# A bidirectional hybrid layer on one core: v by column halves for both token blocks, and the output stage's norms one group ahead

## The chip, the cores and the metric

The kernel runs on one NeuronCore of a Trainium2 chip. The metric is device time in microseconds from the start to the end of one launch on that core; lower is better. TensorE is called PE below, VectorE DVE, ScalarE ACT, GpSimd POOL; SP is the engine that issues most transfers.

## What is computed

One encoder layer on a sequence of 2048 tokens of width 1024, in float32:

```
mod = silu(c) @ w_ada + b_ada;  shift, scale, gate = split(mod)
h = rms_norm(x, norm_g) * (1 + scale) + shift
a, a_glu, a_gate, u, v, b_gate = split(h @ W_in)            # 6 x 1024 columns
y_a = silu(layer_norm(conv31(a * sigmoid(a_glu)) + conv_b)) * silu(a_gate)
y_b = u * (W_s @ layer_norm(v) per chunk of 128 tokens and head + b_s) * silu(b_gate)
out = rms_norm(x + gate * (concat(y_a, y_b) @ w_out), final_g)
```

The layer norm of v runs over all 1024 columns of v; the spatial gate then takes, for each of 8 heads, 128 columns of the normalised v.

## The kernel before

**Precision.** Every float32 operand of the large products is split in two parts, a high one and the rest (`split`: ACT copies to the high part, DVE subtracts), and a product is three matmuls: high by high, high by low, low by high. Each of them is 128x128 by 512 columns. 5664 such matmuls are the body of the program: 768 for v, 3360 for the other five column groups of `W_in`, 1536 for `w_out`.

**Halves and pieces.** The sequence is worked in two halves of 1024 tokens (`hf` 0 and 1), each in two token blocks of 512 (r = 0, 1, also called B0 and B1 of x). From the normalised h, the kernel makes seven combined pieces `H` (names A11, A12, S1, A22, S2, S3, S4, each for k = 0 to 3), and a product of two columns by two token blocks takes seven products of a quarter of the size instead of eight (`unit`, the order of M1 to M7 in `ORDER`). v is not made that way: `v_half` makes it with the tokens on the partitions, from A11 and A12 for r = 0, and from S1 and A22 for r = 1, with the weights B1, B2 and Bd = B2 - B1.

**The opening.** 16 tiles `wa` of 512 KB give shift and scale (`mod_half`, one DVE instruction over 128x1024 for each tile, three buffers of the pool `e`); x of half 0 is squared, summed over rows (`x_rows0`, matmul `pc_x`), and spread over the partitions (`spread`, matmul `pr_x`); `h_scale` and `h_parts` make the pieces H. All of it stands ahead of v's first matmul in the order of PE: both `pc_x` and both `pr_x`.

**v before.** `v_half` runs r = 0 with all 1024 columns in eight banks of PSUM, then r = 1. The weights are loaded, split, written back to DRAM (`dW`), and read again wherever they are used a second time. At a block's end, ACT copies four tiles of v to ring slots, DVE and ACT make mean and variance, ACT normalises four tiles of 128x1024 in place (L327), and four writes of 512 KB go to `dV`. In `gmlp`, head j reads its 128 columns of all eight tiles (`vc`, one buffer, 512 KB) and uses them as matmul weights (`px`).

**The middle.** Units `conv_in`, `gmlp` and `conv_gate` follow for each half. The convolution (`conv`) is 736 DVE instructions, L435, set behind everything else by a low priority; those of half 1 run on into the output stage. Its result goes to `dC`.

**The output stage.** Five groups of token tiles, `GROUPS` (0, 3), (3, 4), (7, 4), (11, 3), (14, 2): first tile and number of tiles. The half of the sum over y_b (called B here, weights `wr_8` to `wr_15`) comes first for groups 1 to 4, its partial sums go to DRAM (`part_out`, `dP`). Group 0 then does B and A in one go (`by_rows`), with the weights `wr_0` to `wr_7` replacing those of B; then groups 1 to 4 do A from the partial sums (`part_in`) tile by tile (`by_tile`), and `out_tile` applies gate, residual and the last norm. The conv layer norm of a group is a generator, `norm(gi)`, in four steps: load and sum `Y`; matmul `pmean`, subtract, square; matmul `pc`, reciprocal root; matmul `pr_cn`, scale, Silu (L551), times the gate. In the loop over groups 1 to 4 the norm of group gi + 1 is run while group gi's tiles are multiplied:

```
        if gi + 1 < len(GROUPS):
            steps.append(norm(gi + 1))
        ys = [y_a(gi, j) for j in range(KC)]
        for t in range(nt):
            ...
            step()
        while steps:
            step()
```

**What sets the order.** Each engine runs its own instructions in order; a scheduler at build time merges the program's pieces by priority into one order for each engine, and an instruction that waits holds up those behind it on its engine. Buffers come from pools: `ct` 4 buffers of 256 KB, `e` 3 of 512 KB, `ring` 8, `raw` 2, and in the output stage `ys` 10.

Of the kernel before, what the change touches and what calls it, by code (L numbers as in the profile page):

```python
# [39 lines left out]
def hybrid_layer_kernel(  # L40
# [126 lines left out]

    def mod_half(k, i):
# [3 lines left out]
        w = ek(f"wa_{k}_{i}")  # L172
        nc.sync.dma_start(w, wa_ss[i * KC + k])
# [21 lines left out]
    def x_rows0(xs, rows, b, fills):  # L195
# [72 lines left out]
    def v_op(typ, k, g, name):  # L268
        key = (typ, k, g)
        s = slot(f"w{name}_{typ}_{k}_{g}")  # L270
        if key in dW:
            nc.sync.dma_start(flat(s), dW[key])
            return s
        part = lambda i: w_v[g, 2 * i + k // 2][:, (k % 2) * NG : (k % 2 + 1) * NG]
        raw = ct(f"rv_{typ}_{k}_{g}")
        nc.sync.dma_start(raw, part(0 if typ == "B1" else 1))
        if typ == "Bd":
            r1 = ct(f"rv1_{k}_{g}")
            nc.sync.dma_start(r1, part(0))
            TT(out=raw, in0=raw, in1=r1, op=ALU.subtract)  # L280
        split(s, raw)
        keep(key, s)
        return s

    def v_half(hf, between=lambda: None):
        for r, pairs in enumerate(((("A11", "B1"), ("A12", "B2")), (("S1", "B1"), ("A22", "Bd")))):
            name = f"v{hf}{r}"
            ps = [[(bank if 2 * t + g < 6 else xbank)(f"pv_{hf}_{r}_{t}_{g}") for g in range(2)] for t in range(4)]
            for k in range(KH):
                for i, (b, typ) in enumerate(pairs):  # L290
                    for g in range(2):
                        s = v_op(typ, k, g, name)
                        st, sp = (k, i) == (0, 0), (k, i) == (KH - 1, 1)
                        for t in range(4):
                            a0, a1 = (H[b, k][:, q, t * P : (t + 1) * P] for q in range(2))
                            nc.tensor.matmul(ps[t][g], a0, s[:, 0, :], start=st, stop=False)  # L296
                            nc.tensor.matmul(ps[t][g], a0, s[:, 1, :], start=False, stop=False)  # L297
                            nc.tensor.matmul(ps[t][g], a1, s[:, 0, :], start=False, stop=sp)  # L298
            if r == 0:
                between()  # L300
            st = sm(f"vst_{name}", 16)
            sums, mean, var = st[:, 0:8], st[:, 8:12], st[:, 12:16]
            sq = sm(f"vsq_{name}", 8)
            vt = []
            for t in range(4):
                v = flat(slot(f"vt_{name}_{t}"))
                for g in range(2):
                    act(v[:, g * NG : (g + 1) * NG], ps[t][g], AF.Copy, accum_out=sums[:, 4 * g + t : 4 * g + t + 1])
                vt.append(v)
# [244 lines left out]
    def yslot(name, n):  # L554
        return ysp.tile([P, 2, NG], F32R, tag="ys", name=name)[:, :, :n]
# [123 lines left out]
    for k in range(KH):  # L679
        x_load(0, xs, k, B0)  # L680
# [219 lines left out]
```

## Time and profile before

| | us |
|---|---|
| median of 2 runs | 1459.81 (1458.77 to 1460.85) |
| the profiled execution | 1461.0 |
| its span, first to last instruction | 1459.2 |
| PE, DVE, ACT busy | 1363.8, 1174.6, 545.6 |
| first matmul of v | 43.5 |
| first matmul of the first unit | 147.5 |
| end of the last matmul, start of the last evacuation | 1451.1 |

The page of the profile gives busy time by engine. Matmuls are pipelined, each shown at some 390 ns, while in a stretch without any gap they start every 228 ns, so a stretch's loss is read by counting its matmuls. The view of stages gives busy time and number of instructions of each engine in a stretch; the view of waits names what an idle engine waited for; the timeline shows instructions in order.

### The profile page before, as it was taken

Reading aid. Unit: us, or ns where it says so; the run is one execution under the profiler, and the core shown is the slowest. Engines: PE = TensorE matmul, PEld = TensorE weight load, DVE = VectorE, ACT = ScalarE, POOL = GpSimd, SP = SyncE. Lnnn points to the kernel's source line nnn. Section 1 sums busy time; section 2 is a strip of 40 time slices with the busy share of each in tenths; the row PEclk is TensorE's granted clock in tenths of the full one; section 3 lists DMA queues with packets and bytes.
Section 4 is the critical chain, followed back from the end, with each engine's and each line's share of the span. In section 5 each row is a group of like instructions: output and inputs, shape, how many; then the busy total and the mean of one; then the engine's idle time right before and its main releaser. Section 6 shows DMA issues by size and latency. Waiting matters only on the chain.

```text
span 1459.2 us, 17680 instructions
## 1 busy us (share of the span) xinstructions
PE 1363.8 (93%) x6036; PEld 1120.7 (77%) x6036; DVE 1174.6 (80%) x1976; ACT 545.6 (37%) x989; POOL 33.7 (2%) x82
## 2 busy tenths in 40 slices
PE   2879999999999999999999999999889999997786
PEld 1667788888888888878888888887668888885675
DVE  7972679999999999866898897967998993477864
ACT  4471733444344443542112222222342341345533
POOL 0000000000000000000000000000000000000000
PEclk9999999999999999999999999999999999998898
DMA  8968897869898897669777999999976348355521
GB/s 291 332 246 295 314 393 273 317 238 375 282 345 293 314 309 263 230 224 379 247 233 252 345 389 376 356 366 331 327 279 241 109 163 325 104 187 174 167 97 68
DMA packets 139851, 395.72 MB, mean 271 GB/s; under 512 B 14897, under 2 KB 49873, under 8 KB 135666
## 3 DMA queue, kind: packets, MB, share of 16 engines
q1 hardware_dynamic: 133618, 369.68, 70.9%
q0 software_dynamic: 6144, 24.93, 4.7%
q8 instruction: 47, 0.77, 0.2%
q14 instruction: 42, 0.34, 0.1%
HBM read 234.65 MB, written 159.91 MB: 270 GB/s over the span
## 4 chain that ended last, share of the span: by engine, by line
PE 87%; DVE 5%; DMA 3%; ACT 3%; issue 1%; SPq 0%; DVEq 0%; ACTq 0%
PE pq_u L363 9%; PE pq_a L363 9%; PE po L593 8%; PE po L594 8%; PE po L595 8%; PE pt_u L363 6%; PE pp_u L363 6%; PE pp_a L363 6%; PE pt_a L363 6%; PE pq_s L363 4%; PE pv L296 3%; PE pv L297 3%; PE pv L298 3%; PE pt_s L363 3%; PE pp_s L363 3%; PE px L484 2%
## 5 line engine op out<-in xcount | busy, mean ns | idle before, releaser
L435 DVE SCALAR_TENSOR_TENSOR acc<-gc,cw_sb,acc 128x496 f32<-128x496 f32 (+1 forms) x496 | 345.9, 745 | 0.7
L593 PE MATMUL po<-wr,y 128*128 128x512 f32 x512 | 206.3, 404 | 29.3 <-ACT y L132 23.7
L594 PE MATMUL po<-wr,y 128*128 128x512 f32 x512 | 204.1, 400 | 0.0
L435 DVE SCALAR_TENSOR_TENSOR acc<-gc,cws,acc 128x496 f32<-128x496 f32 (+1 forms) x240 | 179.7, 749 | 29.1 <-ACT acc L444 25.2
L595 PE MATMUL po<-wr,y 128*128 128x512 f32 x512 | 197.3, 393 | 0.0
L593 PEld LDWEIGHTS po<-wr,y 128*128 128x128 f32 x512 | 99.5, 194 | 54.1 <-ACT y L132 25.8
L594 PEld LDWEIGHTS po<-wr,y 128*128 128x128 f32 x512 | 99.3, 194 | 21.7 <-issue 1.0
L595 PEld LDWEIGHTS po<-wr,y 128*128 128x128 f32 x512 | 97.1, 190 | 21.0 <-issue 0.5
L363 PE MATMUL pq_a<-H_S,w_a_M 128*128 128x512 f32 x384 | 92.9, 390 | 1.1 <-ACT w_a_M L132 1.1
L363 PE MATMUL pq_u<-H_S,w_u_M 128*128 128x512 f32 x384 | 93.7, 391 | 0.0
L363 PE MATMUL pt_u<-H_S,w_u_M 128*128 128x512 f32 x384 | 93.5, 391 | 0.0
L363 PE MATMUL pp_a<-H_A,w_a_M 128*128 128x512 f32 x384 | 92.8, 390 | 0.0
L363 PE MATMUL pp_u<-H_A,w_u_M 128*128 128x512 f32 x384 | 92.5, 390 | 0.0
L363 PE MATMUL pt_a<-H_S,w_a_M 128*128 128x512 f32 x384 | 92.2, 389 | 0.0
L363 PEld LDWEIGHTS pq_a<-H_S,w_a_M 128*128 128x128 f32 x384 | 71.8, 188 | 16.7 <-ACT w_a_M L132 1.5
L363 PEld LDWEIGHTS pt_a<-H_S,w_a_M 128*128 128x128 f32 x384 | 72.1, 188 | 15.0
L363 PEld LDWEIGHTS pp_u<-H_A,w_u_M 128*128 128x128 f32 x384 | 71.9, 188 | 14.9
L363 PEld LDWEIGHTS pp_a<-H_A,w_a_M 128*128 128x128 f32 x384 | 71.8, 188 | 14.9 <-ACT w_a_M L132 0.2
L363 PEld LDWEIGHTS pq_u<-H_S,w_u_M 128*128 128x128 f32 x384 | 71.6, 188 | 14.6
L363 PEld LDWEIGHTS pt_u<-H_S,w_u_M 128*128 128x128 f32 x384 | 71.5, 188 | 14.6
L133 DVE TENSOR_TENSOR w_a_M<-raw_a,w_a_M 128x512 fp32r<-128x512 f32 x56 | 37.8, 688 | 22.3 <-ACT w_a_M L132 21.9
L132 ACT ACTIVATE w_u_M<-raw_u 128x512 fp32r<-128x512 f32 x56 | 34.1, 628 | 53.2 <-issue 14.1
(224 smaller groups left out, 2303.8 us busy)
## 6 DMA issues: line engine op xcount, KB each, us to landing
wv_B<-dW_B SPq DMA_DIRECT2D x32, 512.0 KB, 5.8
dW_o<-ws SPq DMA_DIRECT2D x16, 1024.0 KB, 7.2
wr<-dW_o SPq DMA_DIRECT2D x16, 1024.0 KB, 8.8
wa<-in_wa_ss_dram SPq DMA_DIRECT2D x16, 512.0 KB, 5.7
dW_B<-wv_B SPq DMA_DIRECT2D x16, 512.0 KB, 5.0
raw_a<-in_w_main_dram SPq DMA_DIRECT2D x16, 512.0 KB, 6.3
dV<-vt_v SPq DMA_DIRECT2D x16, 512.0 KB, 7.5
dG<-g SPq DMA_DIRECT2D x16, 512.0 KB, 6.2
```

The costliest lines, as they stand in the source:

```text
L132: act(s[:, 0, :], src, AF.Copy)
L133: TT(out=s[:, 1, :], in0=src, in1=s[:, 0, :].bitcast(F32), op=ALU.subtract)
L296: nc.tensor.matmul(ps[t][g], a0, s[:, 0, :], start=st, stop=False)
L297: nc.tensor.matmul(ps[t][g], a0, s[:, 1, :], start=False, stop=False)
L298: nc.tensor.matmul(ps[t][g], a1, s[:, 0, :], start=False, stop=sp)
L363: mm = lambda w, a, st, sp: nc.tensor.matmul(ps, w, a, start=st, stop=sp, skip_group_check=True)
L435: STT(out=pairs(acc, h), in0=pairs(g[:, i : i + n], at), scalar=tab[:, j, i : i + 1], in1=pairs(acc, h), op0=ALU.mult, op1=ALU.add,)
L484: nc.tensor.matmul(ps[:, t * P : (t + 1) * P], vch[:, 4 * b + t, :], wsj, start=True, stop=True)
L593: nc.tensor.matmul(ps, yh, hi, start=st, stop=False, skip_group_check=True)
L594: nc.tensor.matmul(ps, yh, lo, start=False, stop=False, skip_group_check=True)
L595: nc.tensor.matmul(ps, yl, hi, start=False, stop=sp, skip_group_check=True)
```

## The change

Four parts.

1. **Opening.** Ten of the `wa` tiles get buffers of their own (places of H pieces that are not yet in use), so their loads no longer wait for one of three buffers; the four for k = 0 and 4 and the first weights of v are loaded before B1 of x. `x_rows0` for B1 and the pieces of r = 1 are made between the pieces of r = 0, and v's matmuls are interleaved with them.
2. **v.** For each half of the columns (g = 0, 1), both token blocks run at once in eight banks, in the order (r, k) = (0,0), (0,1), (1,0), (0,2), (1,1), (0,3), (1,2), (1,3). B1, B2 and Bd of a (k, g) are made together from two loads, and used for both blocks. v leaves PSUM unnormalised through a `ct` buffer, is squared there against its mean over 512 columns, and goes to `dV` in pieces of 256 KB. Mean and variance over 1024 columns are put together at the end in `vstat`, and `gmlp` normalises `vc` after it is read: eight ACT instructions of 128x128.
3. **Output stage.** B starts with group 3 by rows, then groups 1, 2, 4, then 0. `wr_8` and `wr_9` are loaded into `raw` buffers before the last unit ends. The norm of a group is run one group earlier: norm(2) during group 0's A, norm(gi + 2) during group gi.
4. **Buffers and queues.** `Y` has its own pool of 8, `pi` one of 2, `ys` is 4, and the first four y of a group take ring slots; the write of a partial sum is issued by ACT instead of SP. Tiles other than the last run j-major, both halves of the columns in turn.

```diff
+    def wa_tile(k, i):
+        if (k, i) not in was:
+            if wa_homes:
+                w = hpool.tile([P, D], F32, tag=wa_homes.pop(0), name=f"wa_{k}_{i}")
+            else:
+                w = ek(f"wa_{k}_{i}")
+            nc.sync.dma_start(w, wa_ss[i * KC + k])
...
+    def v_ops(hf, k, g):
...
+        raw = [ct(f"rv{i}_{k}_{g}") for i in range(2)]
+        for i in range(2):
+            nc.sync.dma_start(raw[i], w_v[g, 2 * i + k // 2][:, (k % 2) * NG : (k % 2 + 1) * NG])
+        out = ss()
+        for i in range(2):
+            split(out[i], raw[i])
+        TT(out=raw[1], in0=raw[1], in1=raw[0], op=ALU.subtract)
+        split(out[2], raw[1])
...
+    def v_half(hf):
...
+        for g in range(2):
+            for n, (r, k) in enumerate(((0, 0), (0, 1), (1, 0), (0, 2), (1, 1), (0, 3), (1, 2), (1, 3))):
+                yield
...
+                for t in range(4):
+                    c = 8 * g + 4 * r + t
+                    v = ct(f"v_{hf}_{r}_{t}_{g}")
+                    act(v, ps[r][t], AF.Copy, accum_out=sums[:, c : c + 1])
+                    nc.sync.dma_start(dV[hf][4 * r + t].rearrange("p j d -> p (j d)")[:, g * NG : (g + 1) * NG], v)
+                    nm = sm(f"vnm_{hf}_{c}", 1)
+                    TS(out=nm, in0=sums[:, c : c + 1], scalar1=-1.0 / NG, scalar2=None, op0=ALU.mult)
+                    act(junk, v, AF.Square, bias=nm, accum_out=sqs[:, c : c + 1])
...
-                act(vt[t], vt[t], AF.Identity, bias=nmr[:, t : t + 1], scale=rs[:, t : t + 1])
-                nc.sync.dma_start(dV[hf][4 * r + t].rearrange("p j d -> p (j d)"), vt[t])
...
@@ gmlp
+        for t in range(NTT):
+            act(vch[:, t, :], vch[:, t, :], AF.Identity, bias=vstat[:, 8 + t : 9 + t], scale=vstat[:, t : t + 1])
...
@@ norm
-            y = slot(f"Y_{gi}_{k}", n).bitcast(F32)
+            y = Yp.tile([P, 2, NG], F32, tag="Y", name=f"Y_{gi}_{k}")[:, :, :n]
...
+    def yslot(name, j, n):
+        return slot(name, n) if j < KH else ysp.tile([P, 2, NG], F32R, tag="ys", name=name)[:, :, :n]
...
+            home = (rawp, "raw") if e % KC < 2 else (wrp, f"wr_{e % KC}")
...
-    ysp = pool("ys", 10, reuse_waits="tile")
+    ysp = pool("ys", 4, reuse_waits="tile")
...
@@ by_rows
+            if j % 2 == 0:
+                step()
...
@@ part_out
-        nc.sync.dma_start(dP[t], st)
+        nc.scalar.dma_start(dP[t], st)
...
-    steps += [norm(0), norm(1)]
-    for n, gi in enumerate((1, 2, 3, 4)):
+    for n, gi in enumerate((3, 1, 2, 4)):
...
+        if n == 0:
+            ps = [banks(t0 + t) for t in range(nt)]
+            by_rows(gi, ps, KC, ys, True, True)
+            for t in range(nt):
+                part_out(t0 + t, ps[t])
+            steps += [norm(0), norm(1)]
+            continue
...
-    by_rows(0, ps, 0, y_a, False, True)
+    ys = [y_a(0, j) for j in range(KC)]
+    steps.append(norm(2))
+    by_rows(0, ps, 0, ys, False, True)
...
-        if gi + 1 < len(GROUPS):
-            steps.append(norm(gi + 1))
         ys = [y_a(gi, j) for j in range(KC)]
+        if gi + 2 < len(GROUPS):
+            steps.append(norm(gi + 2))
...
-        while steps:
-            step()
+        if gi + 1 < len(GROUPS):
+            while gi + 1 in todo:
+                step()
```

Where instructions moved is seen at three places. PE at the last change of group, from group 3 to group 4 (`po_13` is a bank of tile 13, `y_4_0` the first operand of group 4, `pr_cn4` the spreading matmul of group 4's norm). Before:

```order
L595 MATMUL po_13_1_11269<-wr_7_10017,y_3_7_11055 128x512
L540 MATMUL pc_4_11346<-ones_102,sq_4_11146 128x1 x2
L162 MATMUL pr_cn4_11363<-dg_cn4_11361,ones_102 128x256
L593 MATMUL po_14_0_11432<-wr_0_9856,y_4_0_11406 128x512
L594 MATMUL po_14_0_11432<-wr_0_9856,y_4_0_11406 128x512
```

Now, first around `pr_cn4`, then around the first matmul of group 4:

```order
L625 MATMUL po_12_0_11343<-wr_1_10012,y_3_1_11240 128x512
L623 MATMUL po_12_1_11344<-wr_1_10012,y_3_1_11240 128x512
L163 MATMUL pr_cn4_11194<-dg_cn4_11192,ones_102 128x256
L624 MATMUL po_12_1_11344<-wr_1_10012,y_3_1_11240 128x512
...
L625 MATMUL po_13_1_11424<-wr_7_10234,y_3_7_11258 128x512
L623 MATMUL po_14_0_11527<-wr_0_9972,y_4_0_11501 128x512
```

Before, nothing stands between `pr_cn4` and group 4, and it is the same with `pr_cn2` and `pr_cn3` ahead of groups 2 and 3; now 192, 117 and 86 matmuls stand between the three and their groups. `pr_cn2` now stands 24 matmuls behind its `pc_2`, right ahead of group 1's first matmul.

DVE in the opening, near the end of the first pass over k (`s1_2` is a `ct` buffer from which the piece S1 for k = 2 is made, `vnm` the negative mean of a piece of v that has left PSUM, `rv1` raw weights of v). Before:

```order
L133 TENSOR_TENSOR wv00_B2_3_0_665<-rv_B2_3_0_666,wv00_B2_3_0_665 128x512
L133 TENSOR_TENSOR H_S1_1_717<-s1_1_715,H_S1_1_717 128x512
L249 SCALAR_TENSOR_TENSOR s1_3_735<-x0_3_0_174,sh2_106,x0_3_1_175 128x512
L133 TENSOR_TENSOR H_S1_2_727<-s1_2_725,H_S1_2_727 128x512
L254 TENSOR_TENSOR s3_0_744<-x0_0_170 128x512
```

Now:

```order
L299 TENSOR_TENSOR rv1_3_0_602<-rv1_3_0_602,rv0_3_0_601 128x512
L134 TENSOR_TENSOR wv0_Bd_3_0_607<-rv1_3_0_602,wv0_Bd_3_0_607 128x512
L338 TENSOR_SCALAR vnm_0_0_649<-vsum_0_258 128x1
L338 TENSOR_SCALAR vnm_0_1_655<-vsum_0_258 128x1
L265 SCALAR_TENSOR_TENSOR s1_2_672<-x0_S3_173,sh2_106,x0_S2_174 128x512
L338 TENSOR_SCALAR vnm_0_2_661<-vsum_0_258 128x1
L338 TENSOR_SCALAR vnm_0_3_667<-vsum_0_258 128x1
L134 TENSOR_TENSOR H_S1_2_674<-s1_2_672,H_S1_2_674 128x512
L265 SCALAR_TENSOR_TENSOR s1_3_727<-x0_3_0_175,sh2_106,x0_3_1_176 128x512
```

The piece S1 for k = 2 now stands behind the first four evacuations of v, and its `ct` buffer is one that v or its weights have held.

SP in the opening, at the first writes of v's second block. Now:

```order
L138 DMA dW_Bd_0_1_698<-wv0_Bd_0_1_686 128x1024
L336 DMA dV_0_129<-v_0_1_0_0_760 128x512
L336 DMA dV_0_129<-v_0_1_1_0_766 128x512
L336 DMA dV_0_129<-v_0_1_2_0_772 128x512
L336 DMA dV_0_129<-v_0_1_3_0_778 128x512
L494 DMA vc_0_0_2747<-dV_0_129 128x8x128
L295 DMA rv0_1_1_827<-in_w_v_dram 128x512
L365 DMA raw_0_a0_1184<-in_w_main_dram 128x1024
L295 DMA rv1_1_1_828<-in_w_v_dram 128x512
```

Before, at the end of the first block's weights:

```order
L137 DMA dW_B2_3_1_689<-wv00_B2_3_1_684 128x1024
L340 DMA raw_0_a0_1215<-in_w_main_dram 128x1024
L341 DMA raw_0_a0_1215<-in_w_main_dram 128x1024
L272 DMA wv01_B1_0_0_865<-dW_B1_0_0_404 128x1024
L272 DMA wv01_B1_0_1_879<-dW_B1_0_1_423 128x1024
```

Now the load `vc_0_0`, which reads what the eight writes of the first column half have written, stands ahead of the weights of k = 1 for the second column half (`rv0_1_1`); before, no load of v's weights stood behind a read of `dV`.

## Rows read from the trace of the kernel before

**Rows 1.** The page, busy time and share of the span of each engine.

```profile
PE 1363.8 (93%) x6036; PEld 1120.7 (77%) x6036; DVE 1174.6 (80%) x1976; ACT 545.6 (37%) x989; POOL 33.7 (2%) x82
```

**Rows 2.** View of stages: stretch, length, busy us (instructions) by engine, PE clock, DMA share, GB/s.

```profile
0.00:150.00 150.00, 107.48 (x421) 84.10 (x422) 97.45 (x190) 68.85 (x136) 3.36 (x13) 0.97 0.80 287
150.00:1036.00 886.00, 880.18 (x4012) 730.48 (x4011) 761.05 (x1177) 314.69 (x534) 19.59 (x48) 1.00 0.86 310
1036.00:1100.00 64.00, 51.84 (x207) 41.68 (x208) 58.63 (x103) 27.20 (x45) 1.67 (x4) 0.89 0.86 312
1100.00:1300.00 200.00, 200.00 (x878) 163.97 (x877) 147.91 (x250) 65.80 (x128) 3.21 (x6) 1.00 0.53 183
1300.00:1351.00 51.00, 41.73 (x178) 33.76 (x178) 37.31 (x79) 23.58 (x47) 2.13 (x4) 0.90 0.58 183
1351.00:1404.00 53.00, 44.67 (x187) 36.31 (x186) 39.19 (x94) 25.96 (x55) 1.60 (x3) 0.90 0.43 138
1404.00:1459.20 55.20, 37.89 (x159) 30.39 (x157) 33.02 (x89) 19.56 (x47) 2.13 (x4) 0.87 0.24 86
```

**Rows 3.** Timeline, DVE behind the last matmul: start, length, instruction, [idle before, releaser].

```profile
1451.11 0.69 DVE L606 TENSOR_TENSOR tm<-po,gate_b 128x512 f32<-128x512 f32 x1 [1.50 <-PE po L595]
```

**Rows 4.** View of waits, PE: line waited for: us in total, times, longest.

```profile
PE po L593 <- ACT y L132: 23.7, 3, 9.3
PE pr_x L162 <- DVE dg_x L155: 16.3, 2, 12.9
PE pr_cn L162 <- DVE dg_cn L155: 8.9, 2, 5.9
PE po L593 <- DMA wr<-dW_o: 5.6, 1, 5.6
PE pv L296 <- DMA wv_B<-dW_B: 5.1, 2, 2.9
```

**Rows 5.** Timeline, PE at the change from group 1 to group 2.

```profile
1314.79 1.02 PE L162 MATMUL pr_cn<-dg_cn,ones 128*128 128x512 f32 x2
1325.08 0.80 PE L593 MATMUL po<-wr,y 128*128 128x512 f32 x1 [9.27 <-ACT y L132]
```

**Rows 6.** Timeline, DVE and ACT in the same stretch.

```profile
1316.87 4.91 DVE L550 TENSOR_TENSOR Y<-Y,sq 128x512 f32<-128x512 f32 x8 [0.45 <-ACT sq L163]
...
1318.77 5.75 ACT L551 ACTIVATE Y<-Y,cols_sb 128x512 f32<-128x512 f32 x8
```

**Rows 7.** The page: taps of the convolution (busy us, mean ns); a load of `wr` (median us).

```profile
L435 DVE SCALAR_TENSOR_TENSOR acc<-gc,cw_sb,acc 128x496 f32<-128x496 f32 (+1 forms) x496 | 345.9, 745 | 0.7
...
wr<-dW_o SPq DMA_DIRECT2D x16, 1024.0 KB, 8.8
```

**Rows 8.** View of DMA, issues: KB each, median us from issue to landing.

```profile
vc<-dV SPq DMA_DIRECT2D x16, 512.0 KB, 6.9
...
rv_B<-in_w_v_dram SPq DMA_DIRECT2D x16, 256.0 KB, 6.2
```

**Rows 9.** View of lines by form, ACT, the whole span: busy us, mean ns.

```profile
L327 ACT ACTIVATE vt_v<-vt_v,nmr_v,r_v 128x1024 f32<-128x1024 f32 x16 | 18.5, 1231 | 8.7 <-DVE nmr_v L325 8.7
...
L551 ACT ACTIVATE Y<-Y,cols_sb 128x256 f32<-128x256 f32 x8 | 4.0, 587 | 0.0
...
L143 ACT ACTIVATE sd_o<-ov 128x1 f32<-128x1 f32 x16 | 3.2, 200 | 4.0 <-DVE ov L611 3.9
```

**Rows 10.** Timeline, the opening: DVE's third `wa` tile, PE's first matmuls of v.

```profile
17.43 1.22 DVE L174 SCALAR_TENSOR_TENSOR wa<-wa,c_row 128x1024 f32<-128x1024 f32 x1
...
43.52 3.78 PE L296 MATMUL pv<-wv_B,H_A 128*128 128x512 f32 x8 [2.52 <-ACT wv_B L132]
```

**Rows 11.** View of lines by form, DVE, 0 to 150 us: busy us, mean ns.

```profile
L174 DVE SCALAR_TENSOR_TENSOR wa<-wa,c_row 128x1024 f32<-128x1024 f32 x16 | 19.4, 1217 | 0.8 <-DMA wa<-in_wa_ss_dram 0.8
L133 DVE TENSOR_TENSOR H_S<-s,H_S 128x512 fp32r<-128x512 f32 x16 | 10.9, 686 | 2.2 <-ACT H_S L132 2.1
...
L229 DVE SCALAR_TENSOR_TENSOR x<-x,gsc,rows 128x512 f32<-128x512 f32 x12 | 8.5, 744 | 0.0
```

More of the change, by code (lines that the diff above doesn't have):

```diff
@@ L166, in hybrid_layer_kernel @@
     pms = {}
+    wa_homes = [f"H_{b}_{k}" for b in ("S4", "S2", "S3") for k in range(KH) if (b, k) not in (("S2", 3), ("S3", 3))]
+    was = {}
+    def wa_tile(k, i):
[5 more added lines that the diff above has]
+            nc.sync.dma_start(w, wa_ss[i * KC + k])
+            was[k, i] = w
+        return was[k, i]
     def mod_half(k, i):
@@ L206, in x_rows0, with sq @@
             nc.tensor.matmul(pc[:, s : s + 1], acc[:, s * P : s * P + P], ones[:, 0:1], start=True, stop=True)
-        fills[0]()
+        yield
         var = sm(f"var_x{b}", 4)
         TS(out=var, in0=pc[:, :4], scalar1=1.0 / D, scalar2=EPS, op0=ALU.mult, op1=ALU.add)
-        spread(rstd_of(var, 4, f"x0{b}", fill=fills[1]), NG, acc, f"x0{b}")
-        fills[2]()
+        r = rstd_of(var, 4, f"x0{b}", fill=(lambda: mod_half(0, 1)) if b == 0 else nothing)
+        spread(r, NG, acc, f"x0{b}", sq)
+    def sq(name):
+        return sqp.tile([P, D], F32, tag="sq", name=name)
     def x1_square(t):
@@ L265, in piece @@
         return H[b, k]
[L268 to L283, printed above, removed]
@@ L680, in hybrid_layer_kernel, with b1_block @@
         x_load(0, xs, k, B0)
+    for k in (0, KH):
+        for i in range(2):
+            wa_tile(k, i)
     chunks = [xs[k][i] for k in range(KH) for i in range(2)]
     with tc.manual_schedule(engines={mybir.EngineType.DVE}):
[L683 removed]
+        r0 = x_rows0(chunks, rows0, 0)
+        next(r0)
+        mod_half(0, 0)
+        next(r0, None)
+        mod_block(KH)
         h_scale(xs[0], rows0, 0, B0)
         h_parts(xs[0], 0, ("A1",))
+    def b1_block(xs, rows, k):
+        h_scale(xs[k], rows, k, B1)
+        h_parts(xs[k], k, ("S1",))
+    v = v_half(0)
+    next(v)
+    next(v)
     for k in range(KH):
         x_load(0, xs, k, B1)
+    r1 = x_rows0(chunks, rows0, 1)
     for k in range(1, KH):
@@ L690, in hybrid_layer_kernel @@
         mod_block(k + KH)
+        sh2_col(k - 1)
         h_scale(xs[k], rows0, k, B0)
         h_parts(xs[k], k, ("A1",))
-        if k == 2:
-            x_rows0(chunks, rows0, 1, (nothing,) * 3)
-    for k in range(KH):
-        sh2_col(k)
-    def second_block(xs, rows):
-        for k in range(KH):
-            h_scale(xs[k], rows, k, B1)
-            h_parts(xs[k], k, ("S1",))
-        for k in range(KH):
-            h_parts(xs[k], k, ("S2",))
-    v_half(0, lambda: second_block(xs, rows0))
+        next(v)
+        if k == 1:
+            next(r1)
+            next(r1, None)
+        b1_block(xs, rows0, k - 1)
+        next(v)
+    sh2_col(KH - 1)
+    b1_block(xs, rows0, KH - 1)
+    next(v)
+    for k in range(KH):
+        next(v)
+        h_parts(xs[k], k, ("S2",))
+        next(v, None)
     Ys = {}
@@ L714, in hybrid_layer_kernel @@
                 h_parts(xs[k], k, ("A1",))
-            v_half(1, lambda: second_block(xs, rows1))
+                next(v)
+                if k:
+                    b1_block(xs, rows1, k - 1)
+                    next(v)
+            b1_block(xs, rows1, KH - 1)
+            next(v)
+            for k in range(KH):
+                next(v)
+                h_parts(xs[k], k, ("S2",))
+                next(v, None)
         if hf == 0:
```

134 lines of the change are left out of this document (71 added, 63 removed).

## The prediction

> **What bounds the kernel now.** The page's busy times come first: PE 93% and DVE 80% of the span [rows 1]. The reader should not take the 7% that PE lacks for the whole room, nor the 93% at its word, since pipelined matmuls overlap in it. The view of stages tells more: from 1100 to 1300 us PE starts 878 matmuls in 200 us without a gap, 0.228 us each, at full clock [rows 2]. That pace, times a stretch's count, is what the stretch would need. Opening: 150 - 421 x 0.228 = 54 us lost. Middle (where 128-column matmuls spoil the count): PE idle 886 - 880 = 6 us. Start of the output stage: 64 - 207 x 0.228 = 16.8. Then 51 - 178 x 0.228 = 10.4, 53 - 187 x 0.228 = 10.4, and 55.2 - 159 x 0.228 = 18.9, of which 8.1 lie behind the last matmul (1459.2 - 1451.1) [rows 2, 3] and 10.8 ahead of it. In each of the last three stretches the granted clock averages 0.87 to 0.90, that is, part of the stretch runs at 1.2 instead of 2.4 GHz after a stall [rows 2]: a stall costs more than its own length.
>
> The Trainium skill (Perfetto Trace Analysis, Identifying the Most-Contended Engine) holds that weight-load busy share, not matmul busy share, shows the room that is left. Taken alone its 77% [rows 1] would leave 23% or 336 us; but the stretch without a gap shows only 164 of 200, 82% [rows 2], so the room is 1 - 77/82, some 6% or 90 us, and the measurement decides.
>
> The waits name the losses [rows 4]: output matmuls wait three times, 23.7 us together, for ACT's split of y; `pr_x`, in the opening, 16.3; `wr` 5.6 and `pr_cn` up to 5.9 at the start of the output stage. So the bound is PE, with PE waiting for DVE and ACT at both ends of the program.
>
> **Output stage, changes of group.** The timeline of the first change shows the chain: two spreading matmuls at 1314.8, then DVE scales eight Y (4.9 us), ACT runs eight Silu (5.75 us) and splits, and the next group's first matmul starts at 1325.1 [rows 5, 6]: 10.3 us from `pr_cn` to the group. Before, no matmul stands in between. Now 192, 117 and 86 do for groups 2, 3 and 4, which at 0.228 is 44, 27 and 20 us of cover for a chain of about 10 (shorter for group 4, with half the columns). Meanwhile `out_tile` adds for each tile four DVE instructions of 128x512 and one of 128x1024, 4 x 0.686 + 1.2 with [rows 11] as the price, some 5 us with the small ones; two tiles of it and a chain of 7 still fit into 20. The three stretches' 10.4 + 10.4 + 10.8 = 31.6 should go, clock included. New in its place: `pr_cn2` stands 24 matmuls (5.5 us) behind its `pc_2`, ahead of group 1; of the two waits for such a spread now, one is 8.9 - 5.9 = 3.0 [rows 4], so it may cost 0 to 4. I leave 4 for all changes together: gain 27.6.
>
> **Output stage, start.** 16.8 us lost now. `wr_8` and `wr_9` lie in place, the first y too. The other six `wr` of 1 MB follow; by rows, 18 matmuls (4.1 us) use one up. At the median landing of 8.8 us each [rows 7], several at once, wr_10 lands about when it is needed, some 8 to 10 us after the start. At the stretch's 312 GB/s [rows 2] 1 MB takes 3.4 us, less than 4.1. If they come in time, nothing is lost; if one is late, the wait of 5.6 remains. norm(0), which now cost a `pr_cn` wait of up to 5.9, is queued after group 3, about 110 us behind the start; DVE must by then have passed the rest of the convolution; taps at 0.745 [rows 7] and the rest at the prices of [rows 11] come to 101 to 107 us, by my count of DVE's order. So between 0 and 12 of 16.8 remain; I take 6, nearest to one late `wr`. Gain 10.8, bounds 4.8 to 16.8.
>
> **Half 1's v.** Its weights come from `dW`, 24 loads for 32 before in each half; one wait of some 2 us there is gone (5.1 less the longest of 2.9 [rows 4]). Each block of v now leaves PSUM in two parts through four `ct` buffers, which the pieces S1 to S4 and the raw weights use too: a buffer is held until its 256 KB have landed. The rows have 6.2 us for 256 KB of weights, 6.9 for 512 KB of v [rows 8]. In half 1 PE has 48 matmuls (11 us) of the second column half to fill that. Cost -2 to +4; I take +2.
>
> **Reading v normalised.** 16 ACT instructions of 128x1024 (18.5 us) go, 128 of 128x128 come. The rows: 200 ns for one column, 587 for 256 with scale and bias by column [rows 9]; near the middle, say 0.45 us, 58 us in all, 3.6 per unit. ACT is busy 315 of 886 us in the middle [rows 2], so work alone is hidden; where ACT waits in order for the load of `vc`, see the rivals. Cost 0.
>
> **The opening.** v's first matmul at 43.5 [rows 10] waits behind both `pr_x`; now it needs only one, and should start near 24. But DVE sets the pace behind it. Its order is the same up to the tile at 17.4 [rows 10]; from there to the last split of v's weights in the first column half now stand 14 wa tiles, 16 gains, 14 H pieces of that form, 7 sums, 14 splits and 4 subtractions: 14 x 1.217 + 30 x 0.744 + 25 x 0.686 [rows 11] = 56.5, with small ones some 60, less about 0.08 for each overlap: 55. That ends at 72 to 77 us. PE, meanwhile idle in turns, can have done 120 of the 384 matmuls; the other 264 take 60 us, so v could end at 135 without another wait; it ended at 147.4 before, the first unit following at 147.5. Two waits come: S1 for k = 2 takes a `ct` buffer that one of the first four v pieces or the weights held, so its DVE instruction, and those behind it, wait for an evacuation and a 256 KB write, 4 to 7 us by 6.2 [rows 8]; and `rv0_1_1` stands on SP behind `vc_0_0`, which waits for eight writes of v, then takes its own weights' 6.2 and a split: about 4.5 us not covered. Each makes the clock fall for a while, as after the stalls above. 135 + 5.5 + 4.5 + 3 = 148. I take 0 for the opening, with -15 to +15 as its bounds.
>
> **The sum.** 1461.0 (the profiled execution) - 27.6 - 10.8 + 2 + 0 = 1424.6; the median of the runs lies 1.2 below that execution, so 1423.4: **1424 us**, 2.5% faster. By the bounds of the terms the likeliest case runs from 1413 to 1433.
>
> **Rivals.**
>
> *1. The opening gets longer.* For: the four `ct` buffers and SP's order above; DMA is 0.80 busy there [rows 2], so a write may take longer than 6.2. Against: fewer loads of weights. Twelve more us (each of the two waits twice as long): 1436. The Trainium skill (DMA: Bandwidth & Descriptors, Rules for kernel authors) advises transfers of 1 MiB or more, which speaks against v's pieces of 256 KB. The trace agrees so far as 256 KB take 6.2 us and 512 KB 6.9 [rows 8]; by that rule a pair of pieces would cost nearly twice one tile's write, and the 12 us of this rival, not 0, would be the opening's term. Chance 0.17.
>
> *2. DVE becomes the bound of the output stage's first 110 us.* There it must run the rest of the convolution and three groups' splits with 101 to 107 us of work in 110; in the gapless stretch before it was busy 148 of 200 [rows 2]. If waits take 10% of its time, norm(0) is late by about 5 us, norm(1) and the first A weights behind it by as much, with a fallen clock: 12 us back, 1436. Chance 0.15.
>
> *3. The opening gets shorter.* If `ct` buffers come free in time, v ends at 135: 1411. For: the first matmul comes 20 us earlier. Against: DVE's count. Chance 0.13.
>
> *4. Slower: ACT waits for `vc`.* The eight normalising instructions of a head stand on ACT ahead of evacuations that PE needs; `vc` has one buffer, its load is issued when the head before has been multiplied, and lands 6.9 us later [rows 8]. By my count of the order of ACT and PE between two heads, 5.4 us are left beyond that in a unit of 84 matmuls, 19 us. Where the load takes over 12.3 us, ACT holds up PE in each of 16 units; at 16.5 us it is 4.1 x 16 = 66 us: 1490, slower by 2%. For: DMA is 0.86 busy in the middle [rows 2]. Against: a median of 6.9. Chance 0.05.
>
> *5. It does not do what it says.* DVE's order carries splits and the norm's sums mixed with the tiles' evacuations; should the chains be late although issued earlier, the changes of group keep 25 of their 31.6: 1449. Chance 0.05.
>
> **How the numbers follow.** The forecast has 0.45. The range takes in rivals 1, 2, 3 and 5 and the forecast's bounds, and leaves out 4 and the far ends: 1403 to 1452. A difference under 2% is about what a measurement of this kernel can tell from no change; the limit is 1430.6. Faster by more: 0.85 of the forecast, all of rival 3, and a fifth of rivals 1 and 2, 0.38 + 0.13 + 0.06 = 0.57. Slower by more: most of rival 4, 0.04. Within: 0.39.
>
> **What would show it.** In the trace after: three changes of group without a wait for ACT's split of y over 2 us, and a clock of 1.00 over the last 130 us; one wait or none for `wr`; `pr_cn` of norm(0) not waiting over 3 us; v's first matmul near 24 us, but the first unit's still at 140 to 150, with v waiting for DVE's S1 and for weights of k = 1; ACT's 128x128 normalising at 0.3 to 0.6 us each. I am wrong if the first unit starts before 138 or after 158, if the output stage from first to last matmul takes over 380 us instead of 405, or if units in the middle are longer than before.

## The result: 1406.0 us, 3.7% faster, and the profile after

The changed kernel took 1405.97 us (median of two runs, 1404.41 to 1407.54) against 1459.81 before: a ratio of 0.9631, 95% interval 0.9577 to 0.9686. The forecast was 1424, the range 1403 to 1452. The profiled execution took 1404.4 us, with a span of 1401.5, 57.7 less than before.

The page's busy times, to lay beside [rows 1]:

```profile
PE 1354.6 (97%) x6036; PEld 1116.3 (80%) x6036; DVE 1171.6 (84%) x2000; ACT 575.8 (41%) x1099; POOL 33.6 (2%) x82
```

PE executes as many instructions as before. Its 97% must still not be taken for "nothing left": the weight loads stand at 80%, and a gapless stretch shows 163 of 200, 82%, below. The view of stages of the changed kernel, with the columns of [rows 2]:

```profile
0.00:150.00 150.00, 118.73 (x465) 92.97 (x466) 107.61 (x221) 78.89 (x165) 3.34 (x13) 0.94 0.77 287
150.00:1017.00 867.00, 866.32 (x3958) 720.86 (x3958) 771.25 (x1197) 336.66 (x618) 20.30 (x51) 1.00 0.84 303
1017.00:1075.00 58.00, 51.15 (x213) 41.74 (x212) 49.22 (x75) 15.17 (x26) 1.43 (x3) 0.91 0.90 331
1075.00:1275.00 200.00, 200.00 (x881) 163.35 (x880) 145.54 (x256) 85.03 (x149) 1.07 (x2) 1.00 0.53 184
1275.00:1393.40 118.40, 118.36 (x525) 97.40 (x523) 94.21 (x245) 59.12 (x139) 7.44 (x14) 1.00 0.52 179
1393.40:1401.50 8.10, 0.00 (x0) 0.00 (x0) 3.74 (x10) 0.92 (x3) 0.00 (x0) 0.82 0.17 65
```

Three things are to be seen. The last 118 us before the end have no idle time at all and a granted clock of 1.00, where the three last stretches of [rows 2] had 0.87 to 0.90. The start of the output stage (1017 to 1075) is the only stretch behind 150 us that still loses more than 1 us before the last matmul, with a clock of 0.91. And the first 150 us hold 44 more PE instructions than before (465 for 421): v is done earlier. PE's waits, longest first, to lay beside [rows 4]:

```profile
PE pc_x L219 <- DVE rows L216: 11.3, 2, 6.9
PE po L623 <- DMA wr<-dW_o: 6.8, 1, 6.8
PE pv L326 <- ACT wv_B L133: 6.8, 1, 6.8
PE pv L326 <- ACT H_A L254: 4.1, 1, 4.1
PE pr_x L163 <- DVE dg_x L156: 3.6, 2, 3.3
PE pv L326 <- ACT H_S L133: 2.6, 1, 2.6
```

No row of the list names what the changes of group lost: the wait of `po` for ACT's split of y (23.7 us) has gone, and so have `pr_cn` (8.9) and the wait for weights from `dW` (5.1); `pr_x` fell from 16.3 to 3.6, and in its place `pv` waits 6.8 for the split of its weights for k = 2. The wait for `wr` grew from 5.6 to 6.8.

To say where the time came from, the program is cut at PE's own instructions, by their start times in the two traces:

| stretch, cut at PE's matmuls | before | after | difference |
|---|---|---|---|
| start to the first unit of half 0 | 147.45 | 137.32 | -10.1 |
| units of half 0, to the first `pv` of half 1 | 397.75 | 397.54 | -0.2 |
| v of half 1, to its first unit | 92.41 | 89.76 | -2.7 |
| first unit of half 1 to the last `po` | 813.07 | 768.35 | -44.7 |
| behind the last `po` | 8.52 | 8.52 | 0.0 |

### The profile page after: what moved, and what is told of

Its sections match the earlier page's. It is cut to its first block, busy times and chain, and to the rows that moved or that the text cites. A ratio compares the mean times of both kernels' runs of the same rounds, so it can differ in the third digit from the quotient of the medians.

```text
span 1401.5 us, 17779 instructions
## 1 busy us (share of the span) xinstructions
PE 1354.6 (97%) x6036; PEld 1116.3 (80%) x6036; DVE 1171.6 (84%) x2000; ACT 575.8 (41%) x1099; POOL 33.6 (2%) x82
## 4 chain that ended last, share of the span: by engine, by line
PE 94%; DVE 4%; DMA 1%; issue 1%; ACT 0%; SPq 0%; DVEq 0%; ACTq 0%
PE pq_u L388 9%; PE pq_a L388 9%; PE po L623 8%; PE po L625 8%; PE po L624 8%; PE pt_u L388 6%; PE pp_u L388 6%; PE pt_a L388 6%; PE pp_a L388 6%; PE pq_s L388 5%; PE pv L328 4%; PE pv L327 4%; PE pv L326 4%; PE pt_s L388 3%; PE pp_s L388 3%; PE px L512 2%
## 5 line engine op out<-in xcount | busy, mean ns | idle before, releaser
L623 PEld LDWEIGHTS po<-wr,y 128*128 128x128 f32 x512 | 96.8, 189 | 28.7 <-DMA wr<-dW_o 7.3
L624 PEld LDWEIGHTS po<-wr,y 128*128 128x128 f32 x512 | 96.8, 189 | 21.7 <-issue 1.2
L625 PEld LDWEIGHTS po<-wr,y 128*128 128x128 f32 x512 | 96.8, 189 | 20.5
L326 PE MATMUL pv<-wv_B,H_A 128*128 128x512 f32 x128 | 50.6, 416 | 10.9 <-ACT wv_B L133 6.8
L500 ACT ACTIVATE vc<-vc,vstat 128x128 f32<-128x128 f32 x128 | 51.1, 482 | 21.7 <-DMA vc<-dV 19.7
```

The lines of the kernel that those rows point to most:

```text
L326: nc.tensor.matmul(ps[r][t], a0, s[:, 0, :], start=st, stop=False)
L500: act(vch[:, t, :], vch[:, t, :], AF.Identity, bias=vstat[:, 8 + t : 9 + t], scale=vstat[:, t : t + 1])
L623: nc.tensor.matmul(ps, yh, hi, start=st, stop=False, skip_group_check=True)
L624: nc.tensor.matmul(ps, yh, lo, start=False, stop=False, skip_group_check=True)
L625: nc.tensor.matmul(ps, yl, hi, start=False, stop=sp, skip_group_check=True)
```

## Experiments

Each kernel was timed several times beside the kernel before on the same chip; the kernel before had medians of 1460.8 (experiments 1 to 4), 1461.7 (5 to 8), 1462.7 (9) and 1463.9 (10), so times are compared by ratio, or by the milestones of the table above, which come from one profiled execution of each kernel; a difference between two medians in us is subject to that spread of some 3 us. Opening means the time from the start to the first unit's first matmul; output stage means the first unit of half 1 to the last `po`, as in the table.

**1 and 2. Each part alone.** One kernel is the kernel before with the diff's hunks on the opening, on v and on its reading; the other the kernel before with the hunks on the output stage. Their cores:

```diff
 # opening, v and its reading alone
+            if wa_homes:
+                w = hpool.tile([P, D], F32, tag=wa_homes.pop(0), name=f"wa_{k}_{i}")
...
+    v = v_half(0)
```

```diff
 # output stage alone
+            steps += [norm(0), norm(1)]
...
+        if gi + 2 < len(GROUPS):
+            steps.append(norm(gi + 2))
```

> The kernel before with the new opening and the new v (both halves, normalised when read), and the old output stage. Theory: the parts add up; the stages of the two traces say that v of half 0 ends 10.1 us earlier and half 1's v is 2.7 us shorter, so 1459.8 - 12.8 = 1447 us. Rival: the v part only moves waits (evacuation buffers, loads behind vc), and the opening's gain comes with the other buffers of the output stage: within 4 us of 1460.

> The kernel before with the new output stage (order, norms one group ahead, buffers, queue of the partial sums) and the old opening and v. Theory: from half 1's first unit to the last matmul the traces differ by 44.7 us, all of it in this part: 1459.8 - 44.7 = 1415 us. Rival: part of it comes from v (fewer transfers, ACT and DVE freed earlier), then 1420 to 1430.

Measured: 1453.02 (ratio 0.9945, 0.9927 to 0.9964) for the opening and v, 1422.24 (0.974, 0.972 to 0.9761) for the output stage. The opening moved from 147.45 to 138.94 us in the first and stayed at 148.66 in the second; the output stage took 816.5 us in the first, 775.0 in the second. So both parts gain, and each in its own place: about 8 us and 39 us. Both gains are smaller than expected (1447 and 1415), and the second time lies in the range of its rival, that a part of the output stage's gain comes with the new v. PE's waits show what each kept, first of the opening alone:

```profile
PE po L621 <- ACT y L133: 27.3, 6, 9.3
PE po L621 <- DMA wr<-dW_o: 8.3, 1, 8.3
```

and then of the output stage alone:

```profile
PE pr_x L162 <- DVE dg_x L155: 16.5, 2, 13.1
PE po L595 <- DMA wr<-dW_o: 5.5, 1, 5.5
PE po L595 <- ACT y L132: 3.1, 1, 3.1
```

One gain was not where it was thought to be. Half 1's v took 92.4 us in the kernel before, and 90.3 with the output stage alone, whose v is the old one; in the first kernel and every other one with the new v it took 89.8. So one run of the old v differs from another by four times what is left as v's gain, some 0.5 us. The two parts together give 46.4 us, the whole change about 54. The difference stands in the output stage: it is 6.7 us longer in the second kernel than in the changed one (775.0 for 768.35; 3.1 of it is the wait for ACT's split of y in the list above), and 3.4 us longer in the first kernel than in the kernel before. Why these losses come only when the parts are apart was not tried.

**3. The norms not ahead.** In the changed kernel, the norm of each of groups 2 to 4 is run during the group just before it again:

```diff
-    steps.append(norm(2))
...
+        if gi + 1 < len(GROUPS):
+            steps.append(norm(gi + 1))
         ys = [y_a(gi, j) for j in range(KC)]
-        if gi + 2 < len(GROUPS):
-            steps.append(norm(gi + 2))
```

> The changed kernel, but the norm of group gi + 1 runs during group gi again, as before; buffers, order, preloaded weights and queues stay as changed. Theory: the three changes of group cost again what they cost before, 31.6 us less the 0 to 4 that new buffers save: 1406 + 28 to 32 = 1434 to 1438 us, with three waits of output matmuls for ACT's split of y. Rival: the own pool for Y and the ring slots for y are what removed the waits (a split could start before the last group's matmuls ended): then 1406 + 0 to 10.

Measured: 1441.78 (0.9872, 0.9854 to 0.9889), 35.8 us over the changed kernel. The output stage is 805.9 us, 37.5 longer. The stalls are back, by PE's waits:

```profile
PE po L623 <- ACT y L133: 24.9, 3, 9.9
PE po L623 <- DMA wr<-dW_o: 6.8, 1, 6.8
PE pr_cn L163 <- DVE dg_cn L156: 3.7, 1, 3.7
```

28.6 us of waits stand beside 37.5 us of stage. The rest is clock: the view of stages has a granted clock of 0.88 from 1290 us, just ahead of the first of these waits, to the last output matmul, where [rows 2] had 0.87 to 0.90 and the changed kernel has 1.00.

```profile
1290.00:1432.93 142.93, 114.24 (x470) 91.88 (x468) 97.69 (x229) 65.18 (x136) 4.82 (x10) 0.88 0.38 125
```

In PE's timeline of this kernel the spread and the next group's first matmul stand as in [rows 5]:

```profile
1293.82 1.02 PE L163 MATMUL pr_cn<-dg_cn,ones 128*128 128x512 f32 x2
1304.72 0.80 PE L623 MATMUL po<-wr,y 128*128 128x512 f32 x1 [9.88 <-ACT y L133]
```

In PE's timeline of the changed kernel the same norm's spread stands 45 us ahead of group 2's first matmul (1292.4), and an output matmul follows it with nothing between:

```profile
1247.10 0.39 PE L625 MATMUL po<-wr,y 128*128 128x512 f32 x1
1247.33 1.02 PE L163 MATMUL pr_cn<-dg_cn,ones 128*128 128x512 f32 x2
1247.78 0.80 PE L623 MATMUL po<-wr,y 128*128 128x512 f32 x1
```

One edit of the order thus carries 37.5 of the 44.7 us that the stage gained, and the rival, that the new buffers had removed the waits, is out: they were kept here and the waits came back. The expectation of 28 to 32 us was short, since it went by the prediction's 31.6. By PE's timeline the last 500 output matmuls, in which all three changes lie, took 152.2 us from the first to the last in the kernel before, 116.3 in the changed one and 155.1 here: the changes of group lose 35.9 and 38.8 us.

**4. Partial sums' writes on SP.** The queue was changed back for the 13 writes of `dP`, which ACT issues in the change:

```diff
-        nc.scalar.dma_start(dP[t], st)
+        nc.sync.dma_start(dP[t], st)
```

> The changed kernel, but the writes of the partial sums are issued by SP again. Theory: nothing waits for them, 1406 +- 2 us. Rival: on SP each of 13 writes waits for ACT's evacuation and holds up the loads of y and of the weights behind it: 1 to 3 us each where PE is near the loads, 1411 to 1430 us.

Measured: 1406.06 (0.9627, 0.9612 to 0.9641). This edit of the change does nothing for the time that these runs can tell.

**5. Where the opening's waits come from: the queue of the wa loads.**

```diff
+            queue = nc.sync if wa_homes else nc.gpsimd
...
-            nc.sync.dma_start(w, wa_ss[i * KC + k])
+            queue.dma_start(w, wa_ss[i * KC + k])
```

> The changed kernel, but the last six wa loads, which wait for a buffer of three, are issued by POOL instead of SP, so that on SP the weights of v for k = 2 no longer stand behind them. In the trace of the change PE waits 6.8 us there (47 to 55 us) for ACT's split of those weights. Theory: DVE sets the opening's pace (its work up to the last split of v's first weights ends at 72.5 us), so PE starts earlier but catches up with DVE: the first unit starts 0 to 2 us earlier, 1404 to 1406 us. Rival: the SP wait is a real loss: 5 to 7 us earlier, 1399 to 1401.

Measured: 1406.72 (0.9631, 0.9613 to 0.9648), opening 139.94. SP issued the two loads of raw weights at 42.75 us, by its timeline, for 49.19 in the changed kernel:

```profile
42.75 1.24 SPq L296 DMA_DIRECT2D rv<-in_w_v_dram  x2
```

Still `pv` waited 6.3 us for the split of its weights. SP's order there was not the cause.

**6. Where the wait for `wr` comes from.** SP's timeline of the changed kernel (SPq marks transfers that SP issues) shows all six remaining loads of `wr` behind the first group's reads of y and `dS`, a write of the last gate:

```profile
1024.49 3.39 SPq L592 DMA_DIRECT2D y<-dY  x2
1028.19 0.32 SPq L485 DMA_DIRECT2D dS<-sag  x1
1028.56 1.33 SPq L592 DMA_DIRECT2D y<-dY  x2
1029.93 3.87 SPq L617 DMA_DIRECT2D wr<-dW_o  x6
```

In PE's timeline the last matmul that has its weights ends at 1030.48, and the next, which needs the first of these loads, starts 6.85 us later:

```profile
1030.09 0.39 PE L625 MATMUL po<-wr,y 128*128 128x512 f32 x1
1037.32 0.79 PE L623 MATMUL po<-wr,y 128*128 128x512 f32 x1 [6.85 <-DMA wr<-dW_o]
```

The experiment requests two of the six ahead of the first group's y in the program:

```diff
     for e in (KC, KC + 1):
         w_o(e)
+    for e in (KC + 2, KC + 3):
+        w_o(e)
```

> The changed kernel, but the loads of wr_10 and wr_11 are asked for ahead of the y of the first group, so that on SP they stand ahead of the last gate's write and four loads of y. In the trace of the change PE waits 6.8 us for wr_10, whose load is issued only at 1029.9 us, 10 us behind the stage's first matmul, and the clock falls. Theory: the wait is SP's order: some 5 us less wait, 1399 to 1403 us. Rival: DMA is full there (0.9), the loads of y that now come later are waited for instead: 1405 to 1408.

Measured: 1398.58 (0.9568, 0.9554 to 0.9581), 7.4 us less than the changed kernel's 1405.97, and the fastest kernel of this study that computes everything. The output stage took 760.6 us for 768.35. SP now issues two of the six 400 us behind the first unit of half 1 (1026.66 - 626.72) instead of 405.3 (1029.93 - 624.62), ahead of the write of `dS` and of four loads of y, and PE's wait nearly goes, by SP's timeline and by PE's waits:

```profile
1026.66 1.30 SPq L617 DMA_DIRECT2D wr<-dW_o  x2
1030.31 0.32 SPq L485 DMA_DIRECT2D dS<-sag  x1
```

```profile
PE po L623 <- DMA wr<-dW_o: 1.2, 1, 1.2
```

**7. Three `ct` buffers for four.** The prediction let v's pieces compete for these buffers.

```diff
-    ctp = pool("ct", 4)
+    ctp = pool("ct", 3)
```

> The changed kernel with 3 instead of 4 buffers in the pool ct (pieces of v on their way out, raw weights of v, S pieces). It measures how near the buffers are to being a wait, which the prediction priced at 4 to 7 us in the opening. Theory: with four they were just enough, because a write of 256 KB lands before the next use; with three, the opening and half 1's v lose 3 to 6 us each: 1412 to 1418 us. Rival: buffers are not near the path at all: 1405 to 1408.

Measured: 1410.47 (0.9654, 0.964 to 0.9667). The opening took 139.33, as in other kernels with four buffers (138.6 to 139.9), and half 1's v stayed at 89.8; half 1's units took 408.5 us from their first matmul to the last `pq_s` (a matmul of the last unit), for 402.5 to 405.6 in the other kernels with the new v and output stage. So the loss of 4.5 us was smaller than expected, and not in the place; what the units waited for was not followed up. In half 1's v these buffers were not what PE waited for. In the opening they were, a little: DVE's timeline of this kernel has the instruction that makes S1 for k = 2 behind the landing of a write of v,

```profile
81.45 0.75 DVE L265 SCALAR_TENSOR_TENSOR s<-x_S,sh,x_S 128x512 f32<-128x512 f32 x1 [0.63 <-DMA dV<-v]
```

and PE's wait for the piece made from it is 3.3 us, for 2.6 with four buffers.

**8. Normalising twice.** The eight 128x128 instructions of a head are run twice (the second time on data already normalised, so the output's values are other ones):

```diff
             act(vch[:, t, :], vch[:, t, :], AF.Identity, bias=vstat[:, 8 + t : 9 + t], scale=vstat[:, t : t + 1])
+            act(vch[:, t, :], vch[:, t, :], AF.Identity, bias=vstat[:, 8 + t : 9 + t], scale=vstat[:, t : t + 1])
```

> The changed kernel with v's normalising after the read done twice (16 instead of 8 ACT instructions of 128x128 for each of 16 heads; v then comes out scaled twice). It measures the slack that rival 4 was about: 5.4 us by the prediction's count. Theory: 8 x 0.39 = 3.1 us more on ACT for each head stay within the slack: 1405 to 1408 us. Rival: ACT's order is on the path: up to 16 x 3.1 = 50 us, 1410 to 1456.

Measured: 1408.62 (0.9647, 0.9629 to 0.9665). 128 more instructions of 0.48 us, 61 us of ACT, cost 2.7 us by the medians, which the intervals do not tell from nothing. PE's wait behind them was 0.6 us. Normalising v after the read is hidden, with room for as much again.

**9. Half the work of the wa tiles.** DVE multiplies and sums 512 of their 1024 columns, so shift and scale come out wrong; it is a kernel for measuring only:

```diff
-        STT(out=w, in0=w, scalar=1.0, in1=c_row, op0=ALU.mult, op1=ALU.mult, accum_out=pm[:, i : i + 1])
+        STT(out=w[:, :NG], in0=w[:, :NG], scalar=1.0, in1=c_row[:, :NG], ..., accum_out=pm[:, i : i + 1])
```

> Leaves out half of each dot product of the wa tiles (columns 0 to 511 of 1024 are multiplied and summed, loads unchanged), in the changed kernel. It takes DVE work out of the opening: each wa instruction of 128x1024 should fall from about 1.2 us to about 0.7, 16 of them stand ahead of the last split of v's weights, so some 8 us less DVE work. Theory: DVE's count sets when v ends, so first unit 5 to 8 us earlier than the 137.3 to 139.9 of the runs of that opening, and the time 1398 to 1401. Rival: v's end is set by what PE itself must do and by loads of the weights, then the first unit moves by at most 2 us and the time stays 1404 to 1407.

Measured: 1397.36 (0.9547, 0.9522 to 0.9573), 8.6 less than the changed kernel's 1405.97. The opening ended at 129.51, 7.8 us earlier than in the changed kernel's trace, and 9 to 10 earlier than in the other kernels with its opening (138.6 to 139.9). DVE's last split of the first column half, in its timeline, of the changed kernel and then of this one:

```profile
71.85 0.69 DVE L134 TENSOR_TENSOR wv_Bd<-rv,wv_Bd 128x512 fp32r<-128x512 f32 x1 [0.76 <-ACT wv_Bd L133]
```

```profile
62.12 0.68 DVE L134 TENSOR_TENSOR wv_Bd<-rv,wv_Bd 128x512 fp32r<-128x512 f32 x1
```

It comes 9.7 us earlier, and the end of v with it: DVE's count sets the opening. The sixteen instructions themselves fell from 1.216 to 0.684 us each, 8.5 in all.

**10. The same relief without leaving anything out.** On top of experiment 6, six of the sixteen products go to GpSimd, their sums to ACT:

```diff
+        if (k, i) in WA_POOL:
+            nc.gpsimd.tensor_tensor(out=w, in0=w, in1=c_row, op=ALU.mult)
+            act(w, w, AF.Copy, accum_out=pm[:, i : i + 1])
+        else:
```

> Nothing is left out. The kernel with the two w_o requests moved (the version so far fastest, 1398.6), and six of the sixteen wa dot products of the opening (i = 0, k = 1 to 3 and 5 to 7) taken from DVE: GpSimd multiplies the tile by the row, ACT sums it with a Copy. Theory: DVE's count sets v's end in the opening, 6 x 1.22 = 7.3 us less on DVE, about 7 us more on ACT, which is idle there more than half of the time; v ends 4 to 7 us earlier than 138.4 and the time is 1391 to 1396. Rival: the longer way over two engines makes each gain later (GpSimd's multiplication has no price in any row so far), PE waits for H_A instead, and v ends at 137 to 145: 1397 to 1406.

Measured: 1402.61 (0.9582, 0.9564 to 0.9601), no better than experiment 6, and its opening later, at 141.76 for 138.6. The rival's time held, by a cause that it had not named: DVE lost more than it was relieved of. DVE's timeline of this kernel, while GpSimd multiplies:

```profile
26.13 5.67 DVE L260 SCALAR_TENSOR_TENSOR H_A<-x,mod,H_A 128x512 fp32r<-128x512 f32 x2
...
40.13 2.32 DVE L195 TENSOR_TENSOR mod<-pm,bss_sb 128x2 f32<-128x2 f32 x1
42.38 0.68 DVE L135 TENSOR_TENSOR wv_B<-rv,wv_B 128x512 fp32r<-128x512 f32 x1
42.98 2.31 DVE L196 SCALAR_TENSOR_TENSOR gsc<-mod,cols_sb 128x1 f32<-128x1 f32 x1
```

and GpSimd's in the same stretches:

```profile
24.76 9.28 POOL L189 TENSOR_TENSOR wa<-wa,c_row 128x1024 f32<-128x1024 f32 x3 [20.63 <-DMA wa<-in_wa_ss_dram]
40.05 2.38 POOL L189 TENSOR_TENSOR wa<-wa,c_row 128x1024 f32<-128x1024 f32 x1 [6.02 <-DMA wa<-in_wa_ss_dram]
42.73 2.55 POOL L189 TENSOR_TENSOR wa<-wa,c_row 128x1024 f32<-128x1024 f32 x1 [0.29 <-DMA wa<-in_wa_ss_dram]
```

An instruction of two columns lasts 2.32 us, as long as the GpSimd multiplication in which it starts, and ends where that ends (42.45 and 42.43). The two instructions of 128x512 from 26.13 on took 5.67 us, for 1.41 in the changed kernel. DVE was busy 113.0 of the first 150 us, against 107.5 in experiment 6, and its last split of the first column half starts at 76.91 for 71.39 there. The Trainium skill (SBUF — State Buffer, Who interferes with whom) says that a VectorE instruction with two inputs from SBUF contends with a GpSimd instruction that reads SBUF. The Trainium skill (SBUF — State Buffer, Summary: rules for kernel authors) adds that the second of them to start is blocked until the first is done; these rows agree with both.

## Why the prediction was right, and where its sizes were off

The sum was 1424.6 for a profiled execution that took 1404.4. By the table the span fell by 57.7 us, for 36.4 in the sum: the opening gave 10.1 more than forecast, the output stage 6.3 and half 1's v 4.7. All misses lie on one side, so the likeliest case, 1413 to 1433, was missed, and the time lies inside the range by only 3 us, at its low end. That it lies inside is in part luck: the range reached that far down because it took in rival 3, the shorter opening, with a chance of 0.13, and most of that came, on top of an output stage that gained more than its terms.

**Changes of group: right in mechanism, 8 us short.** 27.6 was taken of 31.6, with 4 left for a spread that PE might wait for. Nothing is left: by the stage's rows, 118.4 us hold 525 instructions at 0.228 without a gap. And the room was larger than 31.6: the last 500 output matmuls took 152.2 us and now take 116.3, a gain of 35.9. The prediction's count put every PE instruction of these stretches at 0.228 us, also the norms' matmuls of one column, of which six take 0.73 us together in PE's timeline before; that makes the loss look smaller. Experiment 3 gives the whole mechanism a price of 37.5.

**Start of the output stage: right that one `wr` is late, its clock left out.** The prediction left 6 us here for one late `wr`. The wait is 6.85, the granted clock falls behind it, and by the prediction's own count the stretch still loses 58 - 213 x 0.228 = 9.4 of the 16.8: a gain of 7.4, for 10.8 with bounds of 4.8 to 16.8. Experiment 6 takes 7.7 of the rest. The spread of norm(0) did not wait. The two terms together were 38.4, and the table's stretch measured 44.7; the 1.4 left over (44.7 - 35.9 - 7.4) are within what such a count can place.

**Half 1's v: no cost came.** +2 was taken, between -2 and +4; the table has -2.7, outside these bounds, of which experiment 2 leaves some 0.5 to the change. The buffers that were to cost the 2 us did not bind here: with three of them v takes the same 89.8 us (experiment 7).

**Reading v normalised: right.** 0 was taken; ACT's price was estimated at 0.45 and is 0.482 us, as the page's row says. Experiment 8 shows that rival 4, ACT waiting for `vc`, was far off: twice the work fits too. The load of 512 KB that it was about lands in 5.3 us, not 6.9.

```profile
L500 ACT ACTIVATE vc<-vc,vstat 128x128 f32<-128x128 f32 x128 | 51.1, 482 | 21.7 <-DMA vc<-dV 19.7
...
dV<-v SPq DMA_DIRECT2D x32, 256.0 KB, 3.8
vc<-dV SPq DMA_DIRECT2D x16, 512.0 KB, 5.3
```

**The opening: waits named rightly in part, sized wrongly.** Its frame held: the first matmul of v at 24.26 us (24 said), DVE's last split of the first column half done at 72.5 (72 to 77 said), v at 135 if no other wait came. But on top of 135 stood 13 us for two waits and their clock, which made the term 0; it measured -10.1. The first unit started at 137.32, and at 138.6 to 139.9 in seven other kernels with that opening: close to the 135 of rival 3, which had a chance of 0.13, and below the 140 to 150 of the forecast. The prediction had named a start before 138 as a mark that it is wrong, and the changed kernel's own trace shows that mark. Of the two waits, the first came at 2.6 us in place of 5.5. It was sized by "a 256 KB write, 4 to 7 us by 6.2", the time of a load in an opening where the DMA engines were 0.80 busy [rows 2]. PE's wait for H_S, the piece S1:

```profile
82.79 0.50 PE L326 MATMUL pv<-wv_B,H_S 128*128 128x512 f32 x1 [2.55 <-ACT H_S L133]
```

DVE's timeline shows S1 for k = 2 (line L265) behind the evacuations of v:

```profile
78.95 0.16 DVE L338 TENSOR_SCALAR vnm<-vsum 128x1 f32<-128x1 f32 x1 [6.41 <-ACT v L335]
79.69 0.15 DVE L338 TENSOR_SCALAR vnm<-vsum 128x1 f32<-128x1 f32 x1 [0.58 <-ACT v L335]
81.04 0.75 DVE L265 SCALAR_TENSOR_TENSOR s<-x_S,sh,x_S 128x512 f32<-128x512 f32 x1 [1.19 <-ACT v L335]
```

The row names ACT's evacuation as the one that came last, but the first write of v landed at the same moment: SP's timeline has it issued at 78.95, and the view of DMA from 78 to 100 us has 2.0 us as the median of these writes, with the DMA engines 0.56 busy:

```profile
78.95 2.92 SPq L336 DMA_DIRECT2D dV<-v  x4
```

```profile
dV<-v SPq DMA_DIRECT2D x8, 256.0 KB, 2.0
```

With three buffers the same row names the write (experiment 7). So an evacuation and then a write of 256 KB stand ahead of S1, as the prediction said, though with four buffers the rows cannot tell which of the two came last; the write took a third of its price. Nor did the clock fall behind this wait, for which 3 us had been taken with the other: it is 1.00 from 78 to 100 us. The second wait, 4.5 us for weights behind `vc_0_0` on SP, did not come: SP issued the four last writes from 92.72 to 95.57 and the load of `vc` at 97.43, and PE is busy without a gap from 100 to 150. So 135 + 2.6 is what stands: 137.6, for 137.32 measured. Rival 1's 12 us failed for the same reason. The Trainium skill's advice of 1 MiB or more for each transfer (DMA: Bandwidth & Descriptors, Rules for kernel authors) had spoken for that rival. It agrees with the rows in the price, 3.8 us for 256 KB and 5.3 for 512 KB over the whole run, but PE hardly waits for it here.

**Rival 2, DVE as the bound of the first 110 us of output,** did not come: no `pr_cn` is among PE's waits, and PE is gapless from 1075 us on. The other two marks of being wrong did not show: the output stage takes 373.5 us from its first to its last matmul, under 380, and the units are no longer than before, 397.5 us for 397.8 in half 0.

## What to carry to other kernels

Where one engine's chain stands between two groups of matmuls, move the chain a whole group ahead and count the matmuls that now cover it; here the clock that no longer fell was worth a third again of the waits that went (37.5 us for 28.6). Price a transfer by a row from a stretch with as much DMA traffic as the one it will run in, and ask first who waits for it. Where a row names one cause of a wait, look whether another came at the same time. Count a stretch's loss by its large matmuls alone. When a gain is left at a start of a stage, read the issuing queue in order of time: here two requests moved up by two lines of code were worth another 7 us.

## What the runs showed of the hardware

GpSimd's multiplication of 128x1024 took 2.8 us on average, and DVE's instructions beside it, all with two inputs, stood still for it: 2.31 us for one column, which takes 0.15 otherwise. An idle GpSimd was thus no free helper for DVE.

After a wait of 6.85 us in the changed kernel, PE's matmuls started 0.43 us apart from 1037.9 to 1043.5 us and 0.23 apart behind that, which are the clock's two levels of 1.2 and 2.4 GHz; the granted clock averaged 0.72 over 1027 to 1045:

```profile
1027.00:1045.00 18.00, 11.15 (x37) 8.62 (x36) 16.49 (x25) 3.73 (x7) 0.00 (x0) 0.72 0.92 354
```

So the wait cost 7.7 us of stage, although experiment 6 did not remove it entirely. Behind the wait of 1.2 us that is left there, and behind the one of 2.55 us in the opening, the granted clock stayed at 1.00 (1027 to 1045 and 78 to 100 us).
